# Moving the copies of expert windows, the mask of the spatial weights and the split of the modulation between TensorE and VectorE

## Chip, core and metric

One core of a Trainium2 chip runs the whole program. The metric is the device time of one execution in microseconds (us), the median of several runs. TensorE (PE) multiplies, VectorE (DVE), ScalarE (ACT) and GpSimd (POOL) do elementwise work, SyncE (SP) issues the loads of weights, and 16 DMA engines move the data. Each engine works through its own instructions in order and waits on semaphores for the others.

## What is computed

Two blocks, one after the other, on 512 tokens of width 2048, all in fp32. The first block projects its input to q, k, v, gates, an indexer and a state-space branch; each block of 128 queries attends only to the keys that the indexer picked; the two branches are joined, projected and normalised. The second block is modulated by a vector `c`, mixes with spatial gating and a second attention, and ends in 32 experts of which each token uses two. Cut to what the change touches:

```python
q, k, v, z_attn, q_idx, k_idx, w_idx, z_ssd, xbc, dt_raw = _split_cols(u, IN_WIDTHS)
o_attn = _dsa_attention(q, k, v, q_idx, k_idx, w_idx) * jax.nn.silu(z_attn)
...
mod = silu(c) @ w_mod + b_mod + mod_layer            # [1, 2048] @ [2048, 12288]
shift1, scale1, gate1, shift2, scale2, gate2 = jnp.split(mod, 6, axis=-1)
...
w = ws * jnp.tril(jnp.ones((128, 128)))              # spatial gating
s = jnp.einsum('gtp,bcpgk->bctgk', w, v) + bs.T[:, :, None]
...
act = jax.nn.silu(xb @ w_gate[e]) * (xb @ w_up[e])   # each expert, on its rows
y = act @ w_down[e]
x = x + gate2 * m
```

## The kernel before

**Products.** An fp32 product is made of three faster ones: ACT casts a raw weight tile to a high part `wh` (L123), DVE subtracts it to get the low part `wl` (L124), and PE multiplies high by high, high by low and low by high (L148 to L150, `mm3`). A weight chunk is 256 rows by 512 columns, 1 MB; `gemm` loads one chunk after another into four raw tiles, and after each chunk calls `bg`, which advances the modulation in the background.

**First block.** It starts with the projections for the indexer (two halves of 8 chunks), then k and v, the queries of head group 0, the queries of head group 1 and the z gates (8 chunks each, 16 for z). The picking of keys runs on DVE. `attend` (L690 to L707) is called for each head group and each block of 128 queries: scores on PE (L690), mask and maximum on DVE (L692, L694), exponential on ACT, normalisation on DVE (L698), transposes on PE (L203), a split of the transposed probabilities `pT` by ACT and DVE, and the product with the values on PE. The convolution and state-space branch follow; its load of the decay table, `m<-ac_d` (L554), is an SP instruction.

**Modulation.** `modulation` is a generator whose string `plan` says for each 512 KB tile of `w_mod` whether PE or DVE reduces it; `bg` takes two tiles for a weight chunk. A P tile (`mod_pe`, L289) is four matmuls whose stationary operand is one column of `c_silu`, into four strips of one PSUM tile `m`; 32 P tiles make 2048 columns, closed by L295. A D tile (`mod_dve`, L320) is two multiply-adds over 128x512 on DVE into `macc`; 8 D tiles make 512 columns. Each D section is begun with a POOL memset (L309) and an SP load (L310), and ended with a matmul by ones (L326), an ACT copy and an ACT store (L328). Every tile is loaded by SP (L276) into the buffer `wm` or into one of the raw tiles that the weights use too.

**Experts.** An expert's rows are gathered in `xg`; `expert_up` (L1192) copies its window of 96 rows into one of two buffers `win`, half of it by DVE and half by ACT (both L1199), multiplies by gate and up weights (L1178, L1180, PSUM `s`), and `gathered` (L1188, L1189) takes the result out: three ACT copies and a DVE sum, called `gu`. `expert_mid` makes `h` (ACT L1219, DVE L1220) and its transpose `hT` (ACT L1225). `expert_down` multiplies by the down weights into PSUM `g` (four tiles) and takes that out: `yt` by ACT (L1188), `y` by DVE (L1267, L1269); then it scatters. PE's order is up(e), down(e-1), transposes of e. The weights are eleven 1 MB tiles in rotation, loaded by SP (L1168).

**Order.** A list scheduler sets the order of each engine's instructions when the program is built; `issue_after` binds an instruction to stand behind another.

Of the kernel before, what the change touches and what calls it, by code (L numbers as in the profile page):

```python
# [103 lines left out]
class Kern:  # L104
# [148 lines left out]
    def modulation(self):  # L253

        nc, p = self.nc, self.modp
        c = self.const.tile([128, KT], F32, name='c_in')
        nc.sync.dma_start(c, self.a['c'])
        c_silu = self.const.tile([128, KT], F32, name='c_silu')
        nc.scalar.activation(c_silu, c, AF.Silu)
        self.mod = self.dram.tile([1, 12 * 1024], F32, name='mod')  # L260
        self.ones = self.const.tile([128, 1], F32, name='ones')
        nc.vector.memset(self.ones, 1.0)
        pe, dve = self.mod_pe(c_silu), self.mod_dve(c_silu)

        plan = ('PP', 'DD') * 4 + ('PP', 'PD') * 4 + ('PP',) * 16 + ('PP', 'PD') * 4 + ('DD',) * 16 + ('PP', 'DD') * 16 + ('DD',) * 8
        self.mod_n = 0
        for x in ''.join(plan):
            next(pe if x == 'P' else dve)
            self.mod_n += 1
            yield  # L270
# [8 lines left out]
    def mod_pe(self, c_silu):  # L279

        nc = self.nc
        rows = [slice(32 * j, 32 * j + 1) for j in range(4)]
        for s in range(3):
            ps = self.psm.tile([128, 512], F32, tag='m', name='m')
            for b in range(2):
                for k in range(KT):
                    w = self.mod_tile(self.a['w_mod'][s, b, k]).rearrange('p h (j n) -> p (h j) n', j=2)
                    for j in range(4):
                        nc.tensor.matmul(ps[rows[j], b * 256:b * 256 + 256], lhsT=c_silu[:, k:k + 1], rhs=w[:, j, :],  # L289
                                         start=b == 0 and k == 0, stop=False, tile_position=(0, 32 * j))  # L290
                    if b == 1 and k == KT - 1:
                        t = self.wtile('raw', F32, 512, 4, 2, False).rearrange('p k n -> p (k n)')
                        nc.sync.dma_start(t[0:8, 0:640], self.a['mod_add'][s])
                        for j in range(4):
                            nc.tensor.matmul(ps[rows[j]], lhsT=t[0:8, 512 + 32 * j:513 + 32 * j], rhs=t[0:8, 0:512],  # L295
                                             start=False, stop=True, tile_position=(0, 32 * j))
                        for j, row in enumerate(rows):
                            c = (4 * s + j) * 512
                            nc.scalar.copy(t[row, 0:512], ps[row])
                            nc.scalar.dma_start(self.mod[:, c:c + 512], t[row, 0:512])  # L300
                    yield

    def mod_dve(self, c_silu):

        nc = self.nc

        def begin(s):
            acc = self.modq.tile([128, 512], F32, tag='macc', name='macc', bufs=2)
            nc.gpsimd.memset(acc, 0.0)  # L309
            nc.sync.dma_start(acc[0:2], self.a['mod_add2'][s])  # L310
            return acc

        new = begin(0)
        for s in range(12):
            acc = new
            for h in range(8):
                w = self.mod_tile(self.a['w_mod2'][s, h])
                for kk in range(2):
                    k = 2 * h + kk
                    nc.vector.scalar_tensor_tensor(acc, w[:, kk, :], c_silu[:, k:k + 1], acc, OP.mult, OP.add)  # L320
                if h == 4 and s < 11:
                    new = begin(s + 1)
                if h == 7:
                    c = (12 + s) * 512
                    ps = self.sps()
                    nc.tensor.matmul(ps[0:1], lhsT=self.ones, rhs=acc, start=True, stop=True)  # L326
                    nc.scalar.copy(acc[0:1], ps[0:1])
                    nc.scalar.dma_start(self.mod[:, c:c + 512], acc[0:1])  # L328
                yield
# [475 lines left out]
    def mixer2(self, b2, op):  # L805
# [17 lines left out]
        gm = self.row_bcast(b2, a['gm_norm_g'], 512, 'gm')  # L823
        ws = b2.tile([128, 4, 128], F32, name='ws')
        nc.sync.dma_start(ws, a['gm_ws'])
        nc.vector.tensor_tensor(ws, ws, self.mask_le[:, None, :].to_broadcast([128, 4, 128]), OP.mult)
        with tc.tile_pool(name='sb', **kw) as sb:
            for b, g, half in ((0, gq, (0, 1)), (1, gk, (0, 1)), (0, gq, (2, 3)), (1, gk, (2, 3))):
                ps = self.gemm('R', a['w_in_2'][b], op, bg=1, toks=half)
# [22 lines left out]
            for b in range(4):  # L852
                nc.sync.dma_start(self.gate1[b], self.mod[:, 4096 + b * 512:4608 + b * 512].broadcast_to([128, 512]))

            ps = self.gemm('R', a['w_in_2'][3], op)
            for i in range(4):
                t = b2.tile([128, 512], F32, tag='row', name='row', bufs=3)
# [325 lines left out]
    def gathered(self, ex, main, ps, tag):  # L1183
# [1 line left out]
        nc = self.nc  # L1185
        t = ex.tile([W, 512], F32, tag=tag, name=tag, bufs=2 if tag == 'gu' else 1)
        for s in (2, 0, 1):
            nc.scalar.copy(t[32 * s:32 * s + 32], ps[s][96:128])  # L1188
        nc.vector.tensor_tensor(t, t, main[0:W], OP.add)  # L1189
        return t  # L1190

    def expert_up(self, ex, e, start, between=()):  # L1192

        nc, a = self.nc, self.a
        if start is not None:
            self.win.append(self.win.pop(0))
            for c in range(2):
                k8 = slice(8 * c, 8 * c + 8)
                (nc.scalar.copy if c else nc.vector.tensor_copy)(  # L1199
                    self.spread(self.win[0][:, k8, :]), self.xg[:, k8, bass.ds(start, W)].rearrange('p k (b a) -> p k b a', a=16))  # L1200
        win = self.win[0]
        u = [self.sps() for _ in range(3)]
        for c in range(4):
# [49 lines left out]
    def expert_down(self, ex, e, hT, ix, wt):  # L1253
# [4 lines left out]
        for q in range(2):  # L1258
# [7 lines left out]
            c = [slice((2 * q + b) * 512, (2 * q + b + 1) * 512) for b in range(2)]  # L1266
            nc.vector.scalar_tensor_tensor(y[:, c[0]], p[0][0:W], wt, self.gate2[0:W, c[0]], OP.mult, OP.mult)  # L1267
            t = self.gathered(ex, p[1], p, 'yt')
            nc.vector.scalar_tensor_tensor(y[:, c[1]], t, wt, self.gate2[0:W, c[1]], OP.mult, OP.mult)  # L1269
            self.last_mm = self.mm  # L1270
        nc.gpsimd.indirect_dma_start(out=a['out'].rearrange('i p d -> (i p) d'),  # L1271
                                     out_offset=bass.IndirectOffsetOnAxis(ap=ix, axis=0), in_=y, in_offset=None,
                                     bounds_check=511, oob_is_err=False, compute_op=OP.add)

    def experts(self):
# [3 lines left out]
        if True:  # L1279
            with tc.tile_pool(name='ex', **kw) as ex:  # L1280
                self.worder = [8, 9, 10, 0]
                tail = [1, 2, 3]
                self.win = [ex.tile([128, KT, W], F32, name='x%d' % n) for n in range(2)]
                self.ybuf = [ex.tile([128, 2048], F32, name='y%d' % n) for n in range(2)]
                self.xg = self.mx.tile([128, KT, 1024 + W], F32, name='xg')
# [36 lines left out]
                    old = (hT,) + self.places(ex, place[:, e:e + 1], past[:, e:e + 1])  # L1322
                self.expert_down(ex, 31, *old)

                n = self.reg(self.novf, mybir.ALL_ENGINES, 15)
                with tc.For_i(0, n) as j:
                    o = ex.tile([128, 8], I32, name='ov')
# [26 lines left out]
def prep(i):  # L1354
# [46 lines left out]
    o['tab_q'] = table(128, 32)  # L1401

    o['c'] = np.ascontiguousarray(_np(i['c_2']).reshape(16, 128).T)
    wm = _np(i['w_mod_2']).reshape(16, 128, 2, 6144)
    o['w_mod'] = np.ascontiguousarray(wm[:, :, 0].reshape(16, 128, 3, 4, 2, 256).transpose(2, 4, 0, 1, 3, 5))
    o['w_mod2'] = np.ascontiguousarray(wm[:, :, 1].reshape(8, 2, 128, 12, 512).transpose(3, 0, 2, 1, 4))
    ma = np.stack([_np(i['b_mod_2']), _np(i['mod_layer_2'])[0]]).reshape(2, 2, 6144)
    o['mod_add2'] = np.ascontiguousarray(ma[:, 1].reshape(2, 12, 512).transpose(1, 0, 2))
    ma = ma[:, 0].reshape(2, 3, 4, 512).transpose(1, 2, 0, 3).reshape(3, 8, 512)
    sel = np.zeros((3, 8, 128), f)  # L1410
    for j in range(8):
        sel[:, j, 32 * (j // 2)] = 1.0
    o['mod_add'] = np.ascontiguousarray(np.concatenate([ma, sel], 2))
# [33 lines left out]
```

## Time and profile before

| | |
|---|---|
| three runs | 2051.75, 2053.63, 2060.27 us (median 2053.63) |
| the profiled execution: time, span of its trace | 2049.85 us, 2048.1 us |
| mean granted TensorE clock | 0.972 of full |
| PE, DVE, ACT, POOL busy | 1894.3, 1268.0, 848.0, 334.7 us |
| first attention, q and z projections | 268.3 to 585.1 us |
| expert loop | about 1480 to 2037 us |

The busy time of PE says how much of the span it had a matmul in flight; what it lost is read from the windows, where busy time stands beside the length of the stretch and the granted clock, and from the waits, which name who released the engine.

### The profile page before, as it was taken

The numbers are of one execution on the slowest core, as the hardware profiler recorded it, in microseconds if no ns is written. First come the engines' busy times: TensorE is split into PE (matmuls) and PEld (weight loads), VectorE is DVE, ScalarE is ACT, GpSimd is POOL, SyncE is SP. The second block draws the span as 40 slices with busy tenths as digits, with TensorE's granted clock in tenths as the row PEclk, the third lists the DMA queues.
The fourth block names the chain that finished last, engine by engine and source line by source line (L and its number), as shares of the span: only waits on it lengthen the run. The fifth ranks groups of instructions, "written<-read, shape, count | busy, mean of one in ns | idle before, by whom it ended". The sixth has DMA issues, their size and how long they took to land. (4 is left out here: it accounts for less than half of the span.)

```text
span 2048.1 us, 30020 instructions
## 1 busy us (share of the span) xinstructions
PE 1894.3 (92%) x11574; PEld 1222.4 (60%) x11574; DVE 1268.0 (62%) x2274; ACT 848.0 (41%) x1418; POOL 334.7 (16%) x255
## 2 busy tenths in 40 slices
PE   8999999887999999999997999889489999999996
PEld 5677766554777778888776888778432322222222
DVE  4868977557577787568886664877633333333332
ACT  3443123423234453434444554545244444444442
POOL 0421144000011101001111120043331111111111
PEclk9999999988999999999998999999799999999998
DMA  8654666136866674476655332655799999999992
GB/s 303 228 197 160 241 228 205 61 105 211 273 215 228 209 271 146 167 285 247 206 204 151 116 120 96 247 196 206 294 360 376 405 395 401 403 389 403 395 394 81
DMA packets 115490, 502.82 MB, mean 246 GB/s; under 512 B 22298, under 2 KB 23834, under 8 KB 84498
## 3 DMA queue, kind: packets, MB, share of 16 engines
q1 hardware_dynamic: 108642, 479.81, 63.7%
q0 software_dynamic: 6080, 16.83, 3.2%
q10 hardware_dynamic: 624, 4.24, 0.5%
q8 instruction: 92, 1.51, 0.3%
q14 instruction: 52, 0.43, 0.1%
HBM read 479.75 MB, written 37.84 MB: 253 GB/s over the span
## 5 line engine op out<-in xcount | busy, mean ns | idle before, releaser
L124 DVE TENSOR_TENSOR wl<-raw,wh 128x1024 fp32r<-128x1024 f32 (+1 forms) x272 | 355.0, 1310 | 214.4 <-ACT wh L123 212.8
L123 ACT CAST wh<-raw 128x1024 fp32r<-128x1024 f32 (+1 forms) x272 | 280.6, 1032 | 467.4 <-PE g L150 206.6
L149 PE MATMUL g<-wl,op 128*128 128x512 f32 (+1 forms) x896 | 351.3, 392 | 6.6 <-DVE wl L124 6.4
L150 PE MATMUL g<-wh,op 128*128 128x512 f32 (+1 forms) x896 | 346.5, 387 | 0.0
L148 PE MATMUL g<-wh,op 128*128 128x512 f32 (+1 forms) x896 | 328.8, 392 | 17.2 <-ACT wh L123 15.1
L148 PE MATMUL g<-op,wh 128*128 128x512 f32 x672 | 270.3, 403 | 1.7 <-ACT wh L123 1.7
L149 PE MATMUL g<-op,wh 128*128 128x512 f32 x672 | 266.1, 397 | 0.0
L150 PE MATMUL g<-op,wl 128*128 128x512 f32 x672 | 261.0, 394 | 0.0
L1178 PE MATMUL s<-wop,x 128*32 128x512 f32 x1710 | 251.4, 593 | 0.0
L1180 PE MATMUL s<-wop,x 128*32 128x512 f32 x570 | 251.0, 593 | 0.0
L148 PEld LDWEIGHTS g<-wh,op 128*128 128x128 f32 x896 | 170.7, 191 | 55.0 <-ACT wh L123 17.5
L149 PEld LDWEIGHTS g<-wl,op 128*128 128x128 f32 x896 | 170.8, 191 | 45.0 <-DVE wl L124 10.4
L150 PEld LDWEIGHTS g<-wh,op 128*128 128x128 f32 x896 | 170.7, 191 | 32.4
L1178 PEld LDWEIGHTS s<-wop,x 128*32 128x32 f32 x1710 | 68.0, 110 | 158.1 <-issue 152.3
L148 PEld LDWEIGHTS g<-op,wh 128*128 128x128 f32 x672 | 126.7, 189 | 51.6 <-issue 21.8
L150 PEld LDWEIGHTS g<-op,wl 128*128 128x128 f32 x672 | 126.5, 188 | 30.1 <-issue 3.5
L1188 ACT COPY gu<-s 32x512 f32<-32x512 f32 x96 | 55.6, 579 | 214.7 <-PE s L1180 214.7
L149 PEld LDWEIGHTS g<-op,wh 128*128 128x128 f32 x672 | 127.0, 189 | 24.4
L1178 PE MATMUL g<-wop,hT 128*32 128x512 f32 x810 | 123.5, 594 | 14.6 <-ACT yt L1188 11.0
L1188 ACT COPY yt<-g 32x512 f32<-32x512 f32 x192 | 111.0, 578 | 49.4 <-DVE y L1269 26.3
L1180 PE MATMUL g<-wop,hT 128*32 128x512 f32 x270 | 123.5, 596 | 0.0
L1189 DVE TENSOR_TENSOR gu<-gu,s 96x512 f32<-96x512 f32 x32 | 21.8, 683 | 145.2 <-ACT gu L1188 145.2
(400 smaller groups left out, 2834.8 us busy)
## 6 DMA issues: line engine op xcount, KB each, us to landing
wop<-in_w_gu SPq DMA_DIRECT2D x95, 1024.0 KB
raw<-in_w_in SPq DMA_DIRECT2D x168, 512.0 KB
wm<-in_w_mod SPq DMA_DIRECT2D x96, 512.0 KB
raw<-in_w_mod SPq DMA_DIRECT2D x96, 512.0 KB
raw<-in_w_out SPq DMA_DIRECT2D x96, 512.0 KB
wop<-in_w_dn SPq DMA_DIRECT2D x45, 1024.0 KB
w<-in_w_gu SPq DMA_DIRECT2D x33, 1024.0 KB
w<-in_w_dn SPq DMA_DIRECT2D x19, 1024.0 KB
```

Source lines behind the costliest of these rows:

```text
L123: nc.scalar.copy(hi, src)
L124: (lo_eng or nc.vector).tensor_tensor(lo, src, hi.bitcast(F32), OP.subtract)
L148: nc.tensor.matmul(out, lhsT=a[0], rhs=b[0], start=start, stop=False)
L149: nc.tensor.matmul(out, lhsT=a[0], rhs=b[1], start=False, stop=False)
L150: nc.tensor.matmul(out, lhsT=a[1], rhs=b[0], start=False, stop=stop)
L1178: nc.tensor.matmul(main[i][32 * s:32 * s + 32], lhsT=xs[i][:, 32 * s:32 * s + 32], rhs=w[i], start=first[i], stop=last[i], tile_position=( ...
L1180: self.mm = nc.tensor.matmul(ps[o][96:128], lhsT=xs[3][:, 32 * o:32 * o + 32], rhs=w[3], start=first[3], stop=last[3], tile_position=(0, 96))
L1188: nc.scalar.copy(t[32 * s:32 * s + 32], ps[s][96:128])
L1189: nc.vector.tensor_tensor(t, t, main[0:W], OP.add)
```

## The change

Three things. In the experts the copies of window e (`win`) are bound behind the last results of an earlier expert on the same engine: `evac[-2]` is, when expert e is built, the last `y` (DVE) and the last `yt` copy (ACT) of down(e-3). The plan of the modulation changes from 96 P and 96 D tiles to 128 P and 64 D: the chunks of the indexer alternate PP and DD, the next 40 chunks (k and v, both query groups, z) have P tiles alone, where before the chunks of the second query group had one D tile in four and the 16 z chunks had only D tiles; the convolution's 32 chunks keep their PP, DD. The tables of columns are cut anew at column 8192. And the masking of `ws` moves in the source behind the router and the loads of gate1.

```diff
-        plan = ('PP', 'DD') * 4 + ('PP', 'PD') * 4 + ('PP',) * 16 + ('PP', 'PD') * 4 + ('DD',) * 16 + ('PP', 'DD') * 16 + ('DD',) * 8
+        plan = ('PP', 'DD') * 8 + ('PP',) * 40 + ('PP', 'DD') * 16 + ('DD',) * 8
...
-        for s in range(3):
+        for s in range(4):
             ps = self.psm.tile([128, 512], F32, tag='m', name='m')
...
-        for s in range(12):
+        for s in range(8):
...
-        nc.vector.tensor_tensor(ws, ws, self.mask_le[:, None, :].to_broadcast([128, 4, 128]), OP.mult)
...
+            nc.vector.tensor_tensor(ws, ws, self.mask_le[:, None, :].to_broadcast([128, 4, 128]), OP.mult)
             ps = self.gemm('R', a['w_in_2'][3], op)
...
-            nc.scalar.copy(t[32 * s:32 * s + 32], ps[s][96:128])
+            self.last_copy = nc.scalar.copy(t[32 * s:32 * s + 32], ps[s][96:128])
...
-                (nc.scalar.copy if c else nc.vector.tensor_copy)(
-                    self.spread(self.win[0][:, k8, :]), self.xg[:, k8, bass.ds(start, W)].rearrange('p k (b a) -> p k b a', a=16))
+                with self.tc.issue_after(self.evac[-2][c].ins) if len(self.evac) > 1 else contextlib.nullcontext():
+                    (nc.scalar.copy if c else nc.vector.tensor_copy)(
+                        self.spread(self.win[0][:, k8, :]), self.xg[:, k8, bass.ds(start, W)].rearrange('p k (b a) -> p k b a', a=16))
...
-            nc.vector.scalar_tensor_tensor(y[:, c[1]], t, wt, self.gate2[0:W, c[1]], OP.mult, OP.mult)
+            last = nc.vector.scalar_tensor_tensor(y[:, c[1]], t, wt, self.gate2[0:W, c[1]], OP.mult, OP.mult)
...
+        self.evac.append((last, self.last_copy))
```

**The attention, SP.** Loads of weights (L136), of modulation tiles (L276), of the decay table (L554) and of a new section's bias (L310), around the first L554. Before:

```order
L136 DMA raw<-in_w_in 128x1024
L276 DMA wm<-in_w_mod 128x1024
L276 DMA raw<-in_w_mod 128x1024
L136 DMA raw<-in_w_in 128x1024
L276 DMA raw<-in_w_mod 128x1024
L554 DMA m<-ac_d 128x2048
L310 DMA macc<-in_mod_add 2x512 x2
L276 DMA wm<-in_w_mod 128x1024
L136 DMA raw<-in_w_in 128x1024
```

Now:

```order
L276 DMA raw<-in_w_mod 128x1024
L276 DMA wm<-in_w_mod 128x1024
L136 DMA raw<-in_w_in 128x1024
L276 DMA raw<-in_w_mod 128x1024
L276 DMA wm<-in_w_mod 128x1024
L554 DMA m<-ac_d 128x2048
L136 DMA raw<-in_w_in 128x1024
L276 DMA raw<-in_w_mod 128x1024
L276 DMA wm<-in_w_mod 128x1024
```

L554 stood behind 60 rows of L136 and stands behind 73 of them; the two L310 behind it are gone from this place.

**The attention, PE.** The last scores (L690) of head group 1 and what follows: `g` is a projection, `s<-pT` the product with the values, L289 a P tile. Before:

```order
L690 MATMUL s<-kT_595,qT 128x512 x3
L203 MATMUL s<-cst,p 128x128 x4
L148 MATMUL s<-pTh,vh 128x512
L203 MATMUL s<-cst,p 128x128 x4
L149 MATMUL s<-pTl,vh 128x512
```

Now:

```order
L690 MATMUL s<-kT_595,qT 128x512
L148 MATMUL g<-op,wh 128x512
L149 MATMUL g<-op,wh 128x512
L150 MATMUL g<-op,wl 128x512
L148 MATMUL g<-op,wh 128x512
L289 MATMUL m<-wm,c_silu 1x256 x2
L203 MATMUL s<-cst,p 128x128
L289 MATMUL m<-wm,c_silu 1x256 x2
L289 MATMUL m<-raw,c_silu 1x256 x4
```

The last query block ran through with no projection between its steps, from the last L690 to the last product with the values; now nearly five chunks of projection stand between those two, and P tiles among them.

**An expert, ACT.** The copies of one expert in the middle of the loop, from one `gu` to the end of its `yt`; the window's copy is L1199 before and L1201 now, `TENSOR_LOAD sc` fetches its start. Before:

```order
L1155 TENSOR_LOAD sc
L1188 COPY gu<-s 32x512 x3
L1199 ISA
L1199 COPY x_11753<-xg 128x8x6x16
L1188 COPY yt<-g 32x512
L1219 ACTIVATE h<-gu 96x256
L1188 COPY yt<-g 32x512 x2
L1225 COPY hT<-s 128x192
L1188 COPY yt<-g 32x512 x3
```

Now:

```order
L1155 TENSOR_LOAD sc
L1201 ISA
L1201 COPY x_11805<-xg 128x8x6x16
L1188 COPY gu<-s 32x512 x3
L1188 COPY yt<-g 32x512
L1221 ACTIVATE h<-gu 96x256
L1188 COPY yt<-g 32x512 x2
L1227 COPY hT<-s 128x192
L1188 COPY yt<-g 32x512 x3
```

The window's copy stood between the `gu` copies and the first `yt`; it now stands behind the last `yt` of the expert before, ahead of `gu`.

**The mask of `ws`, DVE.** The rows around it in the head norms of the second block (L195 to L197), L826 before and L854 now. Before:

```order
L195 TENSOR_TENSOR rs_t<-rs_y 128x4 x2
L196 SCALAR_TENSOR_TENSOR rs_t<-rs_t,hn_ss 128x4
L826 TENSOR_TENSOR ws<-ws,cst 128x512
L196 SCALAR_TENSOR_TENSOR rs_t<-rs_t,hn_ss 128x4
L197 SCALAR_TENSOR_TENSOR rs_y<-rs_t,rs_y 128x4 x2
L195 TENSOR_TENSOR rs_t<-rs_y 128x4
```

Now:

```order
L195 TENSOR_TENSOR rs_t<-rs_y 128x4 x2
L196 SCALAR_TENSOR_TENSOR rs_t<-rs_t,hn_ss 128x4
L854 TENSOR_TENSOR ws<-ws,cst 128x512
L196 SCALAR_TENSOR_TENSOR rs_t<-rs_t,hn_ss 128x4
L197 SCALAR_TENSOR_TENSOR rs_y<-rs_t,rs_y 128x4 x2
L195 TENSOR_TENSOR rs_t<-rs_y 128x4
```

Nothing moved here: the scheduler put the instruction back between the same two.

## Rows read from the trace of the kernel before

**Rows 1.** Busy time by stretch: start:end, length, each engine's busy us, then PEclk, DMA share, GB/s.

```profile
268.30:360.00 91.70, 85.16 (x439) 60.73 (x438) 69.59 (x133) 28.56 (x51) 37.65 (x21) 1.00 0.61 209
...
340.00:468.00 128.00, 105.20 (x408) 73.14 (x407) 74.37 (x163) 44.50 (x86) 6.61 (x5) 0.92 0.28 95
468.00:512.00 44.00, 30.98 (x123) 21.79 (x123) 33.77 (x40) 13.08 (x17) 1.57 (x3) 0.84 0.72 246
512.00:585.10 73.10, 73.10 (x374) 53.79 (x373) 44.45 (x49) 22.55 (x29) 5.69 (x4) 1.00 0.74 255
268.30:585.10 316.80, 278.27 (x1267) 196.61 (x1266) 206.46 (x360) 103.51 (x173) 45.44 (x29) 0.95 0.53 180
```

**Rows 2.** Waits of PE, 268.3 to 585.1: total us, times, longest.

```profile
PE g L148 <- ACT wh L123: 15.1, 5, 12.6
PE s L203 <- DVE p L698: 8.3, 9, 2.0
PE s L203 <- DVE mx L695: 5.8, 3, 2.0
```

**Rows 3.** Waits of SP's queue, 425 to 475.

```profile
SPq L554 <- DVE p L692: 23.3, 1, 23.3
SPq L310 <- DMA mod<-macc: 15.3, 2, 14.0
```

**Rows 4.** Timeline of PE: start, length, the instruction, idle before and its releaser.

```profile
284.76 0.61 PE L289 MATMUL m<-wm,c_silu 128*1 128x256 f32 x8
...
285.74 0.50 PE L148 MATMUL g<-op,wh 128*128 128x512 f32 x1
...
481.01 2.07 PE L148 MATMUL g<-wh,op 128*128 128x512 f32 x4 [12.63 <-ACT wh L123]
...
816.75 1.02 PE L326 MATMUL s<-macc,ones 128*1 128x512 f32 x2
817.70 0.50 PE L150 MATMUL g<-op,wl 128*128 128x512 f32 x1
```

**Rows 5.** Busy time in the second half of the indexer's projection.

```profile
125.00:180.00 55.00, 54.57 (x340) 40.93 (x338) 38.73 (x52) 25.16 (x44) 18.26 (x12) 1.00 0.49 166
```

**Rows 6.** Busy time by stretch in the experts.

```profile
1561.50:1657.00 95.50, 95.50 (x880) 29.15 (x876) 38.34 (x61) 44.16 (x72) 16.96 (x12) 1.00 1.00 395
1657.00:1993.20 336.20, 322.73 (x2925) 94.85 (x2921) 125.47 (x202) 149.22 (x240) 48.27 (x40) 1.00 1.01 397
1993.20:2009.10 15.90, 15.90 (x151) 4.83 (x147) 4.49 (x8) 5.94 (x11) 2.37 (x2) 1.00 0.89 328
```

**Rows 7.** Wait of PE, 1657 to 1993.2.

```profile
PE g L1178 <- ACT yt L1188: 13.5, 20, 0.7
```

**Rows 8.** Timeline of ACT in one expert with the window's copy, and in one without.

```profile
1802.89 1.62 ACT L1199 COPY x<-xg 128x768 f32 x1
1804.53 0.58 ACT L1188 COPY yt<-g 32x512 f32<-32x512 f32 x1
...
1806.70 0.58 ACT L1188 COPY yt<-g 32x512 f32<-32x512 f32 x1 [0.55 <-DVE y L1267]
...
2004.98 0.58 ACT L1188 COPY yt<-g 32x512 f32<-32x512 f32 x1 [0.35 <-PE g L1180]
```

**Rows 9.** Wait of ACT for the products of the next expert, 1657 to 1993.2.

```profile
ACT gu L1188 <- PE s L1180: 141.6, 60, 6.6
```

**Rows 10.** DMA busy tenths and GB/s, 1980 to 2040, in 40 slices of 1.5 us.

```profile
DMA  9999999999998999993000003000000000600050
GB/s 410 388 366 361 333 404 410 415 382 415 382 350 262 366 339 382 328 421 158 0 11 0 0 0 44 0 0 0 0 0 11 0 0 0 88 11 0 0 77 0
```

**Rows 11.** Timeline of PE at the start of the last expert's down product.

```profile
2026.85 0.63 PE L1178 MATMUL g<-wop,hT 128*32 128x512 f32 x3 [1.45 <-ACT hT L1225]
```

**Rows 12.** Timeline of DVE at the mask of `ws`, and of PE after it.

```profile
1093.70 0.69 DVE L826 TENSOR_TENSOR ws<-ws,cst 128x512 f32<-128x512 f32 x1 [3.69 <-DMA ws<-in_gm_ws]
...
1095.20 1.16 PE L203 MATMUL s<-cst,row 128*128 128x128 f32 x4 [11.43 <-DVE row L803]
```

More of the change, by code (lines that the diff above doesn't have):

```diff
@@ L320, in mod_dve @@
                     nc.vector.scalar_tensor_tensor(acc, w[:, kk, :], c_silu[:, k:k + 1], acc, OP.mult, OP.add)
-                if h == 4 and s < 11:
+                if h == 4 and s < 7:
                     new = begin(s + 1)
                 if h == 7:
-                    c = (12 + s) * 512
+                    c = (16 + s) * 512
                     ps = self.sps()
@@ L1282, in experts @@
                 tail = [1, 2, 3]
+                self.evac = []
                 self.win = [ex.tile([128, KT, W], F32, name='x%d' % n) for n in range(2)]
@@ L1323, in experts @@
                 self.expert_down(ex, 31, *old)
+                self.evac = []
                 n = self.reg(self.novf, mybir.ALL_ENGINES, 15)
@@ L1403, in prep @@
     o['c'] = np.ascontiguousarray(_np(i['c_2']).reshape(16, 128).T)
[L1404 to L1410, printed above, removed]
+    wm = _np(i['w_mod_2']).reshape(16, 128, 12288)
+    o['w_mod'] = np.ascontiguousarray(wm[:, :, :8192].reshape(16, 128, 4, 4, 2, 256).transpose(2, 4, 0, 1, 3, 5))
+    o['w_mod2'] = np.ascontiguousarray(wm[:, :, 8192:].reshape(8, 2, 128, 8, 512).transpose(3, 0, 2, 1, 4))
+    ma = np.stack([_np(i['b_mod_2']), _np(i['mod_layer_2'])[0]]).reshape(2, 12288)
+    o['mod_add2'] = np.ascontiguousarray(ma[:, 8192:].reshape(2, 8, 512).transpose(1, 0, 2))
+    ma = ma[:, :8192].reshape(2, 4, 4, 512).transpose(1, 2, 0, 3).reshape(4, 8, 512)
+    sel = np.zeros((4, 8, 128), f)
     for j in range(8):
```

## The prediction

> **What bounds the kernel now.** I read the windows first, stretch by stretch, then the waits of PE in the stretches that the change touches, and then what the queue of the loads waited for there. In the middle of the expert loop PE is busy 322.73 of 336.2 us and in its early part 95.50 of 95.5 [rows 6]; the difference is one wait, twenty times, on ACT's `yt` [rows 7]. From the first scores of the first block to the end of the z projection (268.3 to 585.1) PE is busy 278.27 of 316.80 us at a mean clock of 0.95, so 38.5 us are idle; the loss is in 340 to 512, where the clock is 0.92 and 0.84, and the last part, 512 to 585, is full [rows 1]. Of the idle time 15.1 us is PE waiting for a weight that ACT has just cast, 12.6 of it in one piece, and 14.1 is the attention's own chain, PE behind DVE's maximum and normalisation [rows 2]. The large piece ends at 481.01 [rows 4]; SP's queue shows its origin: the load of the decay table stood 23.3 us for DVE's mask of the last query block, and the two section loads behind it 15.3 more [rows 3]. SP works in order, so all weights stood behind them: DMA share 0.28 in 340 to 468 [rows 1].
>
> **The change, part by part.**
>
> *The window's copy.* Twenty experts have the same row: the ACT copy of 1.62 us begins at 1802.89, directly behind it comes the first `yt`, and the last `yt` that PE's next product needs starts at 1806.70 only, held by DVE's `y`, which stands behind the delayed `h` [rows 8]. PE, with four PSUM tiles for `g`, waits 0.7 us [rows 7]. In the expert without that copy (1993.2 to 2009.1) ACT waits for PE at this place (0.35 us, [rows 8]) and PE is busy 15.90 of 15.90 us; the six early ones take 95.5 / 6 = 15.92 us, the twenty 336.2 / 20 = 16.81 [rows 6]. The price is 0.89 us each, or 17.7; the waits alone say 13.5 [rows 7], and both are kept. At the new place the copy lies ahead of the next `gu`, for which ACT waits up to 6.6 us per expert [rows 9], so 1.62 us is covered there; `gu`, and through it DVE's sum, is queued behind it and would be late only if that cover fell below 1.62. The window is wanted only by the up product after the next, so a whole up product of another expert lies between. The DVE half moves to the end of the `y` in the same way; DVE is busy 125 of 336 us [rows 6]. What is late next is the supply of weights. The twenty experts moved 397 GB/s x 16.81 us = 6.67 MB each; at 15.92 us that asks for 419 GB/s, and the early stretch at that pace had 395 with the DMA engines at 1.00 [rows 6]. So the stock of loaded weights shrinks: 6.67 MB at 397 takes 16.8 us, 0.9 us per expert more than PE would, at most 18 over the twenty; with the early stretch's own 6.29 MB per expert it would be 0. The last weights have landed by about 2008.5 [rows 10] and the last down product, which takes two of them, starts at 2026.85 [rows 11]: 18.3 us of stock for a drain between 0 and 18. It suffices, barely. I take 17.5 and keep 9 (half, the loads set the pace from the middle on) and 19.
>
> [...]
>
> *The plan of the modulation.* In the stretch, SP's two blocks go: L554 stands 13 chunks later, behind the place where PE has done all scores of the attention, and the section loads are gone, so weights arrive during the attention and PE has projections and P tiles between its steps. The sum is made as PE work plus idle time. Work: 278.27 busy, of which some was at half clock. [...] I take 10: 268. Added: 32 P tiles; a pair takes 285.74 - 284.76 = 0.98 us [rows 4], so 15.7, and one strip more to close, at most 1. Removed: the matmuls that close D sections, four fewer in all, 817.70 - 816.75 = 0.95 us each [rows 4], 3.8. Work after: 281. Idle: the part of this stretch in which projections already stood between the attention's steps, 268.3 to 360, was idle 6.5 of 91.7 us [rows 1], 7%; the z projection's last 73 us had none. 7% of the some 230 us of the attention is 16. So 297 against 316.8: 20 us gained. Bounds: idle of 7 us, as if only that first part kept its own, makes 29; if PE's waits on the attention's chain all stay and only the 15.1 for weights go, idle is 23 and the clock gives back half, so 268 + 5 + 13 + 23 = 309, 8 gained.
>
> TensorE's clock was 1.00 in the part with work between, and 0.84 around the gap of 12.6 us [rows 1, 4]. [...]
>
> In the second half of the indexer four tiles go from PE to DVE: PE, busy 54.57 of 55.00, is rid of 2 us, DVE, busy 38.73, gets 8 more operations of which each is under 0.9 us, 6.7 together, and has 16 free [rows 5]. The picking of keys comes behind it on DVE: between 2 gained and 6.7 lost; I take 0. In the convolution the pairing of tiles is as it was.
>
> *The mask of `ws`.* DVE waits 3.69 us for its load and spends 0.69; PE's gap of 11.43 us ends soon after [rows 12]. Had the mask moved, up to 4.4 us could go. The order shows it between the same two instructions, so I take 0; the upper bound stays 4.4.
>
> **Sum.** 2049.85 - 17.5 - 20 = 2012 for an execution like the profiled one. That one lies 3.8 us under the median of the three runs shown and 1.9 under the fastest; I put half of that on top and forecast 2015.
>
> **Rivals.**
>
> 1. *Only the wait for weights goes in the attention.* The chain through DVE and ACT has 14.1 us of PE's waits [rows 2], which work between would cover only if the scheduler's order fits the times; and 13 us of matmuls have been added. Gain 8 in place of 20: 2026. Against it: the first 92 us of the stretch, in that manner, lose 7%.
>
> 2. *The loads become the bound in the experts.* If the drain is the full 0.9 us and the slack of single tiles below that of the last, PE begins to wait for weights about half way: gain 9 in place of 17.5, 2023. For it: DMA share 1.00 and 395 GB/s where 419 are wanted [rows 6]. Against: no wait for a weight in the early experts at the fast pace. With rival 1 together it is 2035. [...]
>
> 3. *The plan does not do what it says.* L554 still waits for DVE in the attention, at its later place, and the weights stop again: idle stays 38.5 and the 13 us of matmuls are on top. The experts gain 17.5: 2047. Against: by my count of the order some eight chunks of projection lie between the last scores on PE and the chunk behind which it is issued, and loads run at most four raw tiles ahead.
>
> [...]
>
> **How the numbers follow.** I give the forecast 0.62 (2004 to 2022), rivals 1 and 2, alone or together, 0.30 (2023 to 2035), rival 3 0.06, rival 4 0.02. The range leaves out rivals 3 and 4, the worst of both others, and at the other end the case in which every bound is at its best (19 + 29 + 4.4, 1998): 2000 to 2034. A change under 0.5%, 10 us, is about what a measurement of this kernel cannot tell from none; the forecast and rivals 1 and 2 all lie beyond that, rival 3 within it. So faster 0.92, same 0.06, slower 0.02.
>
> **What would show it.** Right: the 0.7 us waits of PE on `yt` are gone and the experts take about 15.9 us to the end; no SP wait at L554 over a few us; PE's idle time from the first scores to the end of z between 10 and 20 us, clock 0.98 or more. Wrong: PE rows that wait for DMA or for `wop` in the late experts (rival 2); PE rows behind L698 and L695 as large as before (rival 1); a long wait at L554 with a gap behind it (rival 3); a granted clock under 0.95 in the experts (rival 4); a mask of `ws` at another place beside its neighbours.

## The result and the profile after

The changed kernel took 2020.26 us (median of 4 runs, 2016.77 to 2020.51) against 2054.0 us (4 runs); ratio 0.9826, 95% interval 0.9808 to 0.9844. That is 34 us less; the prediction was 2015. Measured once more beside the last experiments it was 2014.83 against 2049.95, ratio 0.9821 (0.9799 to 0.9844). The profiled execution after has a span of 2018.5 us, 29.6 less than the one before.

The windows of the changed kernel, in the stretches that answer to [rows 1], [rows 5] and [rows 6]; first the attention from its first scores to the convolution's first product, then its first 91 us, the convolution, the indexer's second half, the experts, and the gather ahead of them:

```profile
270.80:560.20 289.40, 282.53 (x1545) 194.78 (x1543) 152.96 (x281) 110.71 (x179) 31.29 (x23) 1.00 0.57 198
270.80:362.00 91.20, 90.42 (x506) 60.53 (x505) 53.17 (x110) 29.56 (x55) 26.02 (x20) 1.00 0.55 190
...
560.20:761.70 201.50, 198.56 (x1027) 151.87 (x1028) 159.31 (x242) 84.72 (x128) 25.69 (x21) 0.97 0.64 221
125.00:182.00 57.00, 56.31 (x333) 43.27 (x332) 42.74 (x61) 26.89 (x48) 19.14 (x13) 1.00 0.50 170
...
1549.50:1995.60 446.10, 446.10 (x4093) 136.52 (x4090) 172.24 (x281) 210.89 (x335) 72.59 (x55) 1.00 1.00 396
1458.20:1505.60 47.40, 41.50 (x321) 23.57 (x321) 14.63 (x25) 17.84 (x27) 16.90 (x17) 0.88 0.93 352
```

The attention's stretch fell from 316.8 to 289.4 us: idle time from 38.5 to 6.9, the clock from 0.95 to 1.00, while PE did more work. DVE's busy time in it fell from 206.46 to 152.96 us. The experts have no idle time at all: 28 of them in 446.1 us, 15.93 each.

The waits of PE in that stretch, in place of [rows 2], and in the loop, in place of [rows 7]:

```profile
PE s L570 <- ACT cu L534: 3.0, 1, 3.0
PE g L148 <- ACT z L404: 3.0, 1, 3.0
PE s L203 <- DVE p L698: 0.7, 1, 0.7
...
PE g L1178 <- ACT yt L1188: 1.5, 1, 1.5
PE g L1178 <- ACT hT L1227: 1.5, 1, 1.5
```

The wait for a cast weight, 15.1 us before, is gone, and so are the attention's own, 14.1 before and 0.7 now. The twenty waits on `yt` are one.

SP's queue around the place where the decay table is loaded, in place of [rows 3]:

```profile
520.06 0.33 SPq L276 DMA_DIRECT2D wm<-in_w_mod  x1
520.48 0.38 SPq L554 DMA_DIRECT2D m<-ac_d  x1
521.63 0.33 SPq L136 DMA_DIRECT2D raw<-in_w_in  x1
```

L554 is issued 0.4 us after the tile ahead of it and followed by the next weight within 1.2 us; it waits for nothing. [rows 3] begin at 425 us and show two stops of the kernel before. Over its whole stretch there is a third and longer one, also at the begin of a D section, from 367.7 to 397.1 us:

```profile
SPq L310 <- DMA mod<-macc: 46.4, 4, 29.4
```

PE ran out of projections behind it, from 385 to 408 us. All three stops are gone: no wait of SP for the attention is longer than 3.9 us in the changed kernel.

ScalarE in one expert, in place of [rows 8]:

```profile
1805.95 1.78 ACT L1188 COPY yt<-g 32x512 f32<-32x512 f32 x3 [2.87 <-DVE y L1271]
1807.75 1.64 ACT L1201 COPY x<-xg 128x768 f32 x1
1809.42 0.32 ACT L1227 COPY hT<-s 128x192 f32<-128x192 f32 x1
1813.54 0.58 ACT L1188 COPY gu<-s 32x512 f32<-32x512 f32 x1 [3.80 <-PE s L1180]
```

The copy of the window stands behind the last `yt`; after it ACT still waits 3.80 us for the next product, so the place is covered.

The supply of weights at the end of the loop, in place of [rows 10]: DMA busy tenths and GB/s from 1950 to 2010 in slices of 1.5 us:

```profile
DMA  9999999999999999999999998754110000600031
GB/s 421 431 437 404 432 388 350 421 431 421 437 431 393 421 426 399 350 410 421 431 410 399 388 410 339 295 197 186 76 33 0 0 0 0 87 0 11 0 55 22
```

and PE at the start of the last down product, in place of [rows 11]:

```profile
1997.32 0.63 PE L1178 MATMUL g<-wop,hT 128*32 128x512 f32 x3 [1.45 <-ACT hT L1227]
```

The last weights land in the slices up to 1995, two or three us ahead of the last down product; before it was 18.3.

The mask of `ws`, in place of [rows 12]: the same wait for its load, 4.06 us against 3.69.

```profile
1076.59 0.69 DVE L854 TENSOR_TENSOR ws<-ws,cst 128x512 f32<-128x512 f32 x1 [4.06 <-DMA ws<-in_gm_ws]
```

### The profile page after: what moved, and what is told of

The parts are those of the page before. It is cut to its first block, busy times and chain, and to the rows that moved or that the text cites. A ratio compares the mean times of both kernels' runs of the same rounds, so it can differ in the third digit from the quotient of the medians.

```text
span 2018.5 us, 30419 instructions
## 1 busy us (share of the span) xinstructions
PE 1909.2 (95%) x11830; PEld 1232.9 (61%) x11830; DVE 1217.5 (60%) x2210; ACT 862.8 (43%) x1426; POOL 325.9 (16%) x251
## 5 line engine op out<-in xcount | busy, mean ns | idle before, releaser
L150 PEld LDWEIGHTS g<-wh,op 128*128 128x128 f32 x896 | 170.8, 191 | 33.4 <-issue 1.1
L1178 PE MATMUL g<-wop,hT 128*32 128x512 f32 x810 | 120.7, 592 | 3.7 <-ACT hT L1227 2.2
L1180 PE MATMUL g<-wop,hT 128*32 128x512 f32 x270 | 120.9, 594 | 0.0
```

What stands on the lines that cost most here:

```text
L150: nc.tensor.matmul(out, lhsT=a[1], rhs=b[0], start=False, stop=stop)
L1178: nc.tensor.matmul(main[i][32 * s:32 * s + 32], lhsT=xs[i][:, 32 * s:32 * s + 32], rhs=w[i], start=first[i], stop=last[i], tile_position=( ...
L1180: self.mm = nc.tensor.matmul(ps[o][96:128], lhsT=xs[3][:, 32 * o:32 * o + 32], rhs=w[3], start=first[3], stop=last[3], tile_position=(0, 96))
```

## The experiments

Theory 1: ScalarE's copy held up the `yt` copies in twenty experts; in the attention SP stood 23.3 and 15.3 us at instructions that wait for the attention itself [rows 3], and the weights behind them stood with it (by its timeline SP issued no weight, L136, between 423.1 and 476.5 us); TensorE paid for 32 more tiles and got back more. The rivals stand with each experiment. Ratios are to the kernel before, on the same chip.

### One part at a time

e1_copies applies the hunks of the expert loop alone, e2_plan those of the plan and its tables alone, e3_mask the moved line alone. e8_act_half binds only ScalarE's half of the copy:

```diff
-with self.tc.issue_after(self.evac[-2][c].ins) if len(self.evac) > 1 else contextlib.nullcontext():
+with self.tc.issue_after(self.evac[-2][c].ins) if c and len(self.evac) > 1 else contextlib.nullcontext():
```

> Only the copies of the expert windows are moved; plan and mask as before. Theory 1 (the ACT copy held the yt copies for 0.88 us in twenty experts, and nothing else in the loop is near a bound): 17 to 18 us less than before, about 2036, every expert at 15.93 us, and the stock of loaded weights shrinks towards the end. Rival (the gather in front of the loop lost 4 us in the changed kernel because of this change): the gain in the loop is the same but 4 us of it are lost between the gather's first transposes and the first expert, 13 us in all, about 2040.

> Only the plan of the modulation is changed; experts and mask as before. Theory 1 (the stop of the loads in the attention was worth 27 us there, and the convolution gives 6 back): 16 to 19 us less than before, about 2036. Rival (half of the changed kernel's gain in front of the experts comes from elsewhere, the mask or the experts' other order): under 12 us. If the gather's loss of 4 us comes with the plan, it shows here as 13 to 15 us.

> Only the mask of ws is moved in the source. Theory 1 (the scheduler puts it back between the same two instructions): no change, within 3 us of before, DVE's wait of 3.7 us for the load at the mask still there. Rival (it moves the load or the wait): up to 4.4 us less.

> The kernel before with only ScalarE's half of the window's copies bound behind the last results of an earlier expert; VectorE's half as before, plan and mask as before. Theory 1 (it is ScalarE's copy in front of the yt copies that delayed PE): the whole 16 us of e1_copies, about 2039, every expert at 15.93 us. Rival (VectorE's half has a part in it): 8 us or less.

| | median, us | ratio, 95% interval |
|---|---|---|
| e1_copies | 2040.22 | 0.9921 (0.9898 to 0.9943) |
| e8_act_half | 2039.05 | 0.9905 (0.9880 to 0.9930) |
| e2_plan | 2041.17 | 0.9924 (0.9897 to 0.9952) |
| e3_mask | 2057.61 | 1.0004 (0.9986 to 1.0021) |

The copies give 0.8%, 16 us, the plan 0.8%, 16 us, the mask nothing; together 32 of the 34 to 36 measured with all three, within the intervals. The last 27 experts of the loop, from the sixth on, in the kernel before, then in e1_copies, in e8_act_half and in e2_plan:

```profile
1577.40:2025.20 447.80, 434.33 (x3948) 129.06 (x3944) 167.89 (x270) 197.90 (x322) 66.32 (x53) 1.00 0.97 382
```

```profile
1584.50:2014.70 430.20, 430.20 (x3948) 131.67 (x3944) 166.61 (x272) 203.36 (x323) 69.95 (x53) 1.00 1.00 397
```

```profile
1580.80:2010.90 430.10, 430.10 (x3946) 131.61 (x3944) 169.24 (x269) 202.92 (x323) 66.18 (x53) 1.00 1.00 397
```

```profile
1578.50:2025.40 446.90, 434.09 (x3947) 129.09 (x3944) 167.59 (x269) 197.95 (x322) 66.78 (x53) 1.00 0.97 382
```

The 17.6 us of the loop come with ScalarE's half alone; VectorE's half is worth nothing that shows. The plan alone shortens the attention's stretch from 316.8 to 293.3 us, with 6.0 us idle:

```profile
270.60:563.90 293.30, 287.26 (x1544) 197.72 (x1542) 150.57 (x280) 110.64 (x179) 30.97 (x23) 0.98 0.57 196
```

The six times of e2_plan lie 19 us apart (2030.86 to 2050.10), and the execution of its trace is the longest of them, no shorter than the profiled one before. From the convolution's first product to the sixth expert it takes 1014.6 us, where the kernel before takes 992.3 and the two executions of the changed kernel 1005.2 and 997.3. So the 16 us rest on the median of six, the trace shows only what the plan does in the attention, and what spreads these times is not known. The mask in e3_mask stands where it stood and waits as it did:

```profile
1097.33 0.69 DVE L854 TENSOR_TENSOR ws<-ws,cst 128x512 f32<-128x512 f32 x1 [4.11 <-DMA ws<-in_gm_ws]
```

The rival in e1_copies and e2_plan is a loss of 4 us in the gather, and the median of e1_copies is the 2040 that it named. Its trace does not show the loss: from the first up product to the sixth expert it takes 98.0 us against 97.2 before (e2_plan 103.0, the two executions of the changed kernel 101.4 and 94.4). Another execution of the changed kernel, e11_after, takes 40.1 us in the gather, less than the 43.4 before; the rows are the gather before, then e11_after's attention and gather:

> The changed kernel again, on the chip of the other three, for the comparison. Both theories: ratio to before within the first interval, 0.981 to 0.984; experts at 15.93 us, the stretch of the attention at 287 to 293 us.

```profile
1474.60:1518.00 43.40, 39.94 (x320) 23.06 (x320) 15.78 (x26) 17.82 (x27) 16.04 (x17) 0.91 1.00 370
```

```profile
271.80:564.00 292.20, 287.18 (x1545) 198.38 (x1543) 154.78 (x283) 110.73 (x179) 32.21 (x24) 0.98 0.56 196
1461.40:1501.50 40.10, 39.14 (x321) 21.76 (x321) 14.57 (x25) 17.63 (x27) 15.94 (x17) 0.95 1.01 383
```

So the 47.4 of the first execution need not come from the change: two executions of one kernel lie on either side of before. The attention's stretch differs by 2.8 us between two executions of one kernel, so no difference of that size is read below.

### What stops the loads in the attention

e4_mix is the kernel before with another deal of its 96 P and 96 D tiles, none of the D tiles in the second query group, but all z chunks DD:

```diff
-plan = ('PP', 'DD') * 4 + ('PP', 'PD') * 4 + ('PP',) * 16 + ('PP', 'PD') * 4 + ('DD',) * 16 + ('PP', 'DD') * 16 + ('DD',) * 8
+plan = ('PP', 'DD') * 8 + ('PP',) * 24 + ('DD',) * 16 + ('PP', 'DD') * 16 + ('DD',) * 8
```

e7_late is the kernel before with the decay table's load bound behind a later weight, and e5_mix_late is e4_mix with the same edit:

```diff
-        nc.sync.dma_start(m, self.ac_d[hs]...)
+        with self.tc.issue_after(self.last_load.ins):
+            nc.sync.dma_start(m, self.ac_d[hs]...)
```

e6_conv_d has the copies of e1_copies and a third deal of 96 and 96, with the attention's chunks PP, the second half of z DD and the convolution mostly DD:

```diff
+plan = ('PP', 'DD') * 8 + ('PP',) * 32 + ('DD',) * 8 + ('PP', 'DD', 'DD', 'DD') * 8 + ('DD',) * 8
```

> The kernel before with as many P and D tiles as it had (96 and 96), but none of the D tiles in the chunks of the second query group; the z chunks keep their D tiles. In the order of the program SP's load of the decay table and the begin of a D section still stand in front of the z weights, and PE's last query blocks still have no projection between their steps. Theory 1 (the stop of the loads is the cause of the idle time): idle time in the attention stays at 30 us or more, time within 4 us of before. Rival (the D tiles' work on DVE during the attention delays its chain): the 14 us of PE's waits on DVE shrink by half and the time by 7 us or more.

> The kernel before, with only the load of the decay table bound behind the last weight load of the convolution's first projection. Theory 1 (two stops stand in a row and end together, the decay table's and then the begin of a D section whose buffer comes free behind the attention): the second takes the place of the first, the weights still come after the last query block, the 12 us gap stays, time within 4 us of before. Rival (the decay table's load alone is the cause): 12 us less or more.

> The plan of e4_mix (96 and 96, no D tiles in the second query group), and the load of the decay table bound behind the last weight load of the convolution's first projection, so that no SP instruction waits for the attention in front of the z weights. The order on PE is that of e4_mix: no projection between the steps of the last query blocks. Theory 1a (the stop of the loads is most of the loss): the 12 us gap in front of the z projection goes, the clock there stays up, and 15 to 22 us less than before. Theory 1b (the order on PE is most of the loss: the chain of the last query blocks has nothing to cover it, and it is the interleaving that brought the gain): the gap shrinks to the casts of the first weights, some 3 us, but the rest of the idle time (20 us) stays, 8 to 14 us less than before. Rival (SP's stop is not what PE waits for): no change against e4_mix, 2051.

> The copies of the windows as in the changed kernel, mask as before, and a plan with 96 P and 96 D tiles as before the change, dealt so that all chunks from k and v to the first half of z have P tiles, the second half of z D tiles, and the convolution one PP in four chunks and DD in the other three. In the order the attention is interleaved with projections as in the changed kernel. Theory 1 (what counts is that no D tile stands in the attention, not how many columns VectorE sums): the attention is as short as in the changed kernel, PE is spared 32 tiles, 15 us, and if VectorE keeps up in the convolution (159 of 201 us busy, 26 us more) the time is 8 to 15 us under the changed kernel, about 2008. Rival (VectorE becomes the bound in the convolution, or its chains are held up behind the tiles): the convolution is 10 to 30 us longer and the time 2020 to 2035.

Idle time is the length of the window from the first scores to the convolution's first product less PE's busy time in it:

| | ratio, 95% interval | stretch, us | idle, us | clock | stops of SP for the attention over 10 us, in order of time (before and changed: the whole stretch; e6_conv_d: from 420 us on; the others: from 400 us on) |
|---|---|---|---|---|---|
| before | 1 | 316.8 | 38.5 | 0.95 | L310 29.4, L554 23.3, L310 14.0 |
| e4_mix | 0.9978 (0.9965 to 0.9992) | 314.7 | 32.6 | 0.94 | L554 51.3, L310 14.3 |
| e5_mix_late | 0.9980 (0.9967 to 0.9994) | 314.3 | 33.4 | 0.95 | L310 65.8 |
| e7_late | 1.0005 (0.9988 to 1.0022) | 320.8 | 37.9 | 0.94 | L310 37.3 |
| e6_conv_d | 0.9893 (0.9870 to 0.9916) | 300.4 | 17.6 | 0.97 | L310 14.5 |
| changed | 0.9826 (0.9808 to 0.9844) | 289.4 | 6.9 | 1.00 | none |

The three kernels in which SP stands 65 to 67 us in all have 32.6 to 38.5 us of idle time, e7_late, with 37.3 us from 400 us on, has 37.9, the one with 14.5 has 17.6, the one without has 6.9. Three of these kernels are the test of the stops. SP's waits from 400 us on in e4_mix, in e5_mix_late and in e7_late:

```profile
SPq L554 <- DVE p L692: 51.3, 1, 51.3
SPq L310 <- DMA mod<-macc: 15.6, 2, 14.3
```

```profile
SPq L310 <- DMA mod<-macc: 67.0, 2, 65.8
```

```profile
SPq L310 <- DMA mod<-macc: 38.5, 2, 37.3
```

With the decay table's load out of the way, SP stands the whole time at the next instruction, the begin of a D section, whose buffer comes free only when ScalarE, behind the attention, has stored the section before. The two late stops were in a row, and without the first the second is as long as both together (37.3 us in e7_late for 23.3 and 14.0 before, 65.8 in e5_mix_late for 51.3 and 14.3 in e4_mix), so taking away the first is worth nothing (e7_late, as expected). PE's longest waits in e5_mix_late:

```profile
PE g L148 <- ACT wh L123: 11.1, 1, 11.1
PE s L203 <- DVE p L699: 8.3, 10, 1.6
```

I expected 8 to 22 us less from e5_mix_late because I had taken the buffer of that section to be long free with this plan; it is not. The time is the one that the rival named, no difference to e4_mix, but the stop had not been taken away, so it tells nothing between 1a, 1b and the rival. e4_mix gives 4 us, a little more than the limit that I had set and less than the rival's 7; its waits on DVE are 12.5 us against 14.1 (8.4 and 4.1), so the four D tiles that it takes out of the second query group are not what delays the attention's chain.

e6_conv_d has projections between the attention's steps, as the changed kernel has, and one stop left, near the attention's end. Its waits of PE in the stretch, and of SP:

```profile
PE g L148 <- ACT wh L123: 12.5, 1, 12.5
PE s L203 <- DVE p L698: 3.6, 2, 2.2
```

```profile
SPq L310 <- DMA mod<-macc: 15.8, 2, 14.5
```

One stop of 14.5 us, one gap of 12.5 us. And where the loads ran on until then, the attention's own waits are 3.6 us and not 14.1: PE had chunks to work on. That speaks to the question that e5_mix_late left, though it is not a clean cut: the stops and PE's order changed together, and no kernel here has the order of before without a stop, or a stop in mid-attention with the order of after.

The time of e6_conv_d, 2034.71 us, is not under the changed kernel's and lies within its rival's range; its experts gained the same 17.6 us. Theory 1 had the attention as short as in the changed kernel, which it is not by 8 to 11 us, for the stop that is left. From the convolution to the second block's first rows it takes 522.3 us, against 510.1 before and 517.9 in the changed kernel: the rival's 10 to 30 us are there only against the kernel before. Against the changed kernel it is 4.4 us, though PE has 16 P tiles fewer there. In the first two of these windows PE is idle for 16.4 us, in the changed kernel's 299.8 for 2.9:

```profile
568.10:747.70 179.60, 171.86 (x863) 133.57 (x864) 140.44 (x225) 80.65 (x125) 23.71 (x21) 0.99 0.57 197
747.70:860.00 112.30, 103.60 (x437) 82.85 (x437) 77.00 (x106) 39.81 (x52) 10.02 (x7) 0.94 0.56 188
860.00:1090.40 230.40, 209.89 (x936) 172.16 (x934) 179.53 (x291) 96.93 (x133) 31.14 (x16) 0.96 0.67 227
```

The 12 us that the next expectation names for it "against the changed kernel's order" are those against the kernel before.

### What a P tile costs, and whether D tiles could take its place later

e9_no_tiles is the changed kernel with `('..',) * 16` for the z chunks (a point advances the plan and does nothing). e10_d_late has the copies of e1_copies, the P tiles of the changed kernel up to z, and 80 D tiles behind it:

```diff
+plan = ('PP', 'DD') * 8 + ('PP',) * 40 + ('DD', 'D.') * 16 + ('DD',) * 16
```

> The changed kernel with no modulation tile at all in the 16 z chunks: the 32 P tiles that stood there are left out, and the columns 6144 to 8191 of the modulation get the values of the 2048 columns before them (the routing is then another one, so the times from the experts on are not compared). Theory 1 (a P tile costs TensorE 0.49 us, and without a D section in the attention nothing stops the loads): from the first scores to the convolution's first product 14 to 17 us less than the changed kernel's 289.4, idle time there under 12 us, no stop of SP for the attention. Rival (the tiles are partly covered by PE's waits): 8 us or less.

> The copies of the windows as in the changed kernel, mask as before, 96 P and 96 D tiles, none of the D tiles in the attention: the indexer's chunks as in the changed kernel, P tiles alone up to the end of z, then DD and a single D in turn in the convolution (48 D tiles), and DD in the 16 chunks behind it (32). PE has 32 tiles less than in the changed kernel, some 16 us. Theory 1 (the attention as in the changed kernel, no stop of the loads; VectorE in the convolution is at 185 of 201 us and its chains are late by part of that): 2 to 12 us under the changed kernel. Rival (VectorE's order is the bound from the convolution on, as in e6_conv_d, where that part lost about 12 us against the changed kernel's order in spite of fewer P tiles): not under the changed kernel, or up to 10 us over it.

The attention's stretch of e9_no_tiles:

```profile
272.10:543.90 271.80, 263.31 (x1291) 194.14 (x1290) 154.08 (x286) 103.22 (x170) 34.84 (x24) 0.98 0.44 152
```

17.6 us less than the changed kernel's first execution and 20.4 less than its second (292.2): 32 P tiles with the strip that they close cost 0.55 to 0.64 us each. That two executions of one kernel differ by 2.8 us here leaves open whether it is more than the 0.52 that the prediction's terms come to (16.7 for 32). The rival, that PE's waits cover part, falls. SP's longest wait for the attention, from 380 to 520 us, was 6.6 us, not none, and the idle time is 8.5 us. Its time as a whole, 1991.16 us, is not compared, since its routing is another.

e10_d_late took 2027.13 us, ratio 0.9887 (0.9867 to 0.9906), 12 us more than the changed kernel beside it with 32 P tiles fewer. Its windows, the attention, the convolution with the chunks behind it, and the next stage to the second block's first rows:

```profile
270.10:560.70 290.60, 285.92 (x1489) 202.85 (x1487) 170.18 (x307) 110.35 (x179) 31.30 (x23) 0.99 0.57 201
560.70:860.00 299.30, 269.18 (x1210) 212.85 (x1211) 233.36 (x352) 120.65 (x175) 34.48 (x29) 0.95 0.54 183
860.00:1091.50 231.50, 211.86 (x950) 173.39 (x948) 180.61 (x293) 98.84 (x135) 31.29 (x16) 0.97 0.67 235
```

The attention is as in the changed kernel. The two windows behind it take 530.8 us; the changed kernel has 299.8 and 218.1 there, 517.9, with 297 of the first 300 us busy on PE. PE's waits in e10_d_late from 560 to 870:

```profile
PE s L203 <- DVE xs L622: 9.7, 2, 8.5
PE g L148 <- ACT wh L123: 8.2, 6, 4.0
PE s L590 <- DVE m L575: 6.5, 2, 6.3
```

VectorE, 78% busy, is late for the convolution's own chains (`xs` and `m`), and the casts of weights are late too: the rival held, a little beyond its 10 us. Here what the chain of the stage needs from VectorE was late at 78%, before VectorE was full.

### How near the supply of weights is

e12_seven keeps seven of the eleven weight tiles in rotation:

```diff
-                        self.worder += tail + [4, 5, 6, 7]
+                        self.worder += [4, 5, 6]
```

> The changed kernel with seven of the eleven weight tiles in rotation from the second expert on, so some 10 us less stock of loaded weights. Theory 1 (at 15.93 us an expert the DMA engines are past what they can supply, some 16.6 us an expert, and the stock pays the difference, about 15 us over the loop): the stock runs out after some 15 to 20 experts, PE then waits for weights, the last experts take about 16.5 us, 4 to 10 us more than the changed kernel. Rival (the DMA engines have speed in hand and the stock shrinks only because nothing hurries them): no change, under 2 us.

It took 2022.59 us, ratio 0.9874 (0.9851 to 0.9897), 7.8 us more than the changed kernel beside it. The loop in two parts:

```profile
1557.60:1800.00 242.40, 241.16 (x2212) 73.19 (x2212) 92.19 (x151) 115.61 (x183) 39.67 (x30) 1.00 1.01 401
1800.00:1996.10 196.10, 191.13 (x1744) 56.95 (x1732) 71.75 (x119) 86.88 (x141) 30.57 (x23) 1.00 0.99 397
```

and PE's waits in it:

```profile
PE g L1178 <- DMA wop<-in_w_dn: 2.5, 3, 1.4
PE g L1178 <- DMA w<-in_w_dn: 1.7, 2, 1.1
PE g L1178 <- ACT hT L1227: 1.4, 1, 1.4
PE s L1178 <- DMA wop<-in_w_gu: 1.1, 1, 1.1
```

With less stock PE waits for weights, most of it in the second part (idle 5.0 of 196 us against 1.2 of 242), and the rate stays at 397 to 401 GB/s: the loads ran no faster where PE waited for them. The granted clock stayed at 1.00 through these waits of at most 1.4 us. The same 27 experts take 438.5 us, 8.3 more than the 430.2 of e1_copies. The rival falls.

## Why the prediction was right, and where its sum was off

**The copies.** Forecast 17.5; measured 16 (0.0079 of 2055), and 17.6 in the loop of e1_copies. The mechanism, ScalarE's half in front of `yt`, is shown by e8_act_half. The doubt about the weights was well placed: at the end of the loop the stock is some 3 us where it was 18.3, a drain of 15 where the prediction allowed up to 18, and e12_seven shows that with four tiles less in rotation the gain is about halved. Rival 2 did not come true by 3 us.

**The rate of the loads.** The loop ran at 396 to 402 GB/s on one core, under the 419 that the prediction worked out for 15.92 us an expert. The nearest thing here to a ceiling is what e12_seven held while PE waited for weights, 397 to 401.

**The plan, in the attention.** The mechanism held, with one stop more than the prediction saw: it names two blocks of SP, and the longest, 29.4 us, is a third. Work afterwards was forecast at 281 and is 282.5 (287.2 in e11_after, at a clock of 0.98). The terms behind it are less exact than their sum. The stretch got 36 P tiles more and not 32, since the second query group has 16 for 12 and z has 32 for none (the indexer has four fewer), some 2 us; and of the matmuls that close D sections five are gone from it and not four, 1 us the other way.

Idle time was forecast at 16, by the 7% of the first 92 us [rows 1], and is 6.9 (5.0 in e11_after): this is the term that was mis-sized, and it lies below the 10 to 20 us that were to show the prediction right. Those 92 us had waits of their own that went as well: the same part is now idle 0.8 of 91.2 us. The measured value is the lower bound that I had set (7). The clock came back, from 0.95 to 1.00 and 0.98. No run shows the 10 us that the sum takes off PE's work for it; what the trace of the kernel before shows, in slices of 0.5 us, is a granted clock of 0.50 for 34.1 us of the stretch, with PE busy for 20.0 of them, and the changed kernel's first execution has 1.00 in every slice. Of the matmuls below, the first two stand at 0.50 and start 0.43 us apart, the last two at 1.00 and 0.23 apart (kernel before), so by estimate some 9 us of the 20.0 came back:

```profile
482.88 0.63 PE L149 MATMUL g<-wl,op 128*128 128x512 f32 x1
483.31 0.63 PE L150 MATMUL g<-wh,op 128*128 128x512 f32 x1
...
486.12 0.39 PE L150 MATMUL g<-wh,op 128*128 128x512 f32 x1
486.35 0.39 PE L149 MATMUL g<-wl,op 128*128 128x512 f32 x1
```

So the stretch gained 27.4 (24.6 by e11_after) where 20 was forecast.

What the prediction calls the z projection's last 73 us, 512 to 585, is the convolution's first projection: z's last four chunks, whose weights SP had stopped, run from 481 to 508 us. Nothing in the sum hangs on that name.

**The plan, elsewhere.** The indexer cost 2.5 us up to the first scores, where I had put 0 between 2 gained and 6.7 lost; the convolution took 201.5 us against 195.4:

```profile
585.10:780.50 195.40, 192.20 (x1015) 146.57 (x1015) 157.63 (x241) 82.74 (x126) 27.13 (x21) 0.99 0.67 230
```

Half of that is the boundary: by the count of records PE had 12 more matmuls of projections, half a chunk, to do after the convolution's first product than before, some 3 us. The rest fits the time at the lower clock, mean 0.97 against 0.99: in slices of 0.5 us the granted clock is 0.50 for 10.2 us of the one stretch and 3.4 us of the other, by estimate worth some 3 us at the distances of 0.43 and 0.23 us above. Why the clock was lower there is not shown. I had put 0 there because the pairing of tiles is the same. At the convolution's end the plan is worth 18.8 us, and as a kernel of its own, e2_plan, 16: the net of 20 was nearly right because two errors cancel, which is luck.

**The mask.** 0, as the order said.

**The sum.** 2015 for 2020.26 and, in the second comparison, 2014.83; as a gain on the profiled execution 37.5 was forecast, and 29.5 was measured between the two profiled ones and 34 to 36 on the medians. Rivals 1 and 3 did not come true: the chain's waits are 0.7 us and L554 waits for nothing. The kernel was not slower either (rival 4 in the chances): the experts ran at clock 1.00, in e12_seven too, where PE waited up to 1.4 us for weights.

**What stays open.** How much of the 32 us of idle time was the stops of the loads themselves and how much the order of PE that the scheduler made of it; why e4_mix is 4 us under the kernel before; and why the times of e2_plan spread as they do.

## What to carry to other kernels

When one queue issues all loads in order, read what it waits for over the whole stage, and then what the instruction behind that would wait for: stops in a row that end together have to go together, for removing one moved the wait to the next (37.3 us at L310 in e7_late, 65.8 in e5_mix_late). Do not begin a buffer in the middle of work that keeps busy the engines that free it (29.4 us at L310 in the kernel before). A copy that nobody needs for a whole stage belongs behind the results that somebody waits for on the same engine, in the place where that engine itself waits (3.80 us here); when the loop is shortened so, check how much stock of loaded data the shortening uses up (15 us here).

## What the runs showed of the hardware that was not expected

- The loads of the expert loop ran at 395 to 402 GB/s on one core with the DMA share at 0.99 to 1.01, whether an expert took 16.81 or 15.93 us; at 15.93 the stock at the loop's end was 15 us smaller.
- The mean granted clock of the attention's stretch was 0.97 with one gap of 12.5 us and few others (e6_conv_d, 17.6 us idle in all), 0.94 to 0.95 with one of 11.1 to 12.7 us and many of up to two (before, e4_mix, e5_mix_late, 32.6 to 38.5 us idle) and in e7_late (37.9 us idle), and 0.98 to 1.00 in the five executions with 4.7 to 8.5 us of idle time (the changed kernel twice, e2_plan, e9_no_tiles, e10_d_late). In the expert loop of e12_seven gaps of up to 1.4 us went with 1.00.
- Two executions of one kernel differ by 7 us in the gather (47.4 and 40.1) without a change in its order.
